# Softmax over 64 MB: stores moved to Pool's software descriptors, with each engine's share of a store requested as one packet

## Chip, cores, metric

One core of a Trainium2 chip. The metric is device time in microseconds of one execution. "Span" is the profiled time from the first to the last instruction, some 2 us shorter. DVE is VectorE, ACT is ScalarE, Pool is GpSimd and SP is SyncE.

## The reference, cut

```python
x = randn(32, 512, 1024), float32;  temperature = 0.5
scaled  = x / temperature
shifted = scaled - max(scaled, axis=-1)
out     = exp(shifted) / sum(exp(shifted), axis=-1)
```

That is 16384 rows of 1024 elements, 67.11 MB in and 67.11 MB out.

## The kernel before

The rows form 16 tiles of 4.19 MB (128 partitions x 8 rows x 1024 elements). In DRAM the 8 rows of a partition are adjacent, so each partition moves 32 KB in one piece. Six buffers hold tiles; the result overwrites the input in place, and a buffer is loaded anew when its store has landed. Each tile is computed as two groups of four rows.

```python
def load():                       # issued by SP, hardware descriptors
    i = len(tiles)
    if i < len(TILES):
        xt = data.tile([P, sum(TILES[i]), d], f32, name="xt")
        nc.sync.dma_start(out=xt, in_=dram(xf, i))                    # L61
        tiles.append(xt)
# maximum(g): DVE tensor_reduce (L70) and bias (L73); exponential(g): ACT (L79)
# divide(g):  DVE reciprocal (L91) and four tensor_scalar_mul (L93)
def store(g):                     # issued by ACT, hardware descriptors
    i, _, _, part = groups[g]
    if part:                      # after the second group of a tile
        a, k = part
        nc.scalar.dma_start(out=dram(of, i)[:, a : a + k, :],
                            in_=tiles[i][:, a : a + k, :])            # L101
        if a + k == sum(TILES[i]):
            load()
# ... cut ...
for _ in range(BUFS): load()      # BUFS = 6
for g in range(len(groups) + 1):
    if g < len(groups): maximum(g); exponential(g)
    if g > 0:           divide(g - 1); store(g - 1)
```

## Time and profile before

| quantity | before |
|---|---|
| time, median | 318.2 us |
| span | 316.0 us |
| DVE, ACT busy | 75%, 47% |
| DMA queues q1 (loads), q10 (stores) | 49.7%, 49.2% of 16 engines |
| store and load, issue to landing, median | 38.6 us, 50.2 us |

The last row of the table is longer than the 9.7 us that a tile takes at the plateau of 433 GB/s: loads and stores are in flight together and several of each are queued (a store is issued every 19.4 us in the middle of the kernel and takes 38.6 to land). The busy digits of the page, the queue shares and the end of the timeline stand in the prediction, with their reading.

### The profile page before, as it was taken

What the parts mean: (1) busy time and instruction counts of PE and PEld (TensorE: products, weight loads), DVE (VectorE), ACT (ScalarE), POOL (GpSimd) and SP (SyncE); (2) the same over time, 40 slices, a digit from 0 to 9 for tenths busy, and PEclk for the clock granted to TensorE, in tenths of its full rate; (3) what the DMA queues carried; (4) which work ended last, traced back from release to release, by engine and by line L of the source; (5) the groups of instructions that cost most, each with busy time, mean ns of one, the idle gap of its engine ahead of it and who ended that gap; (6) DMA issues with size and microseconds to landing.
All of it is one profiled execution on the core that took longest, in us unless ns stands there. A gap on an engine that the chain in (4) does not pass through costs nothing.

```text
span 316.0 us, 620 instructions
## 1 busy us (share of the span) xinstructions
DVE 235.5 (75%) x224; ACT 149.6 (47%) x257; POOL 0.2 (0%) x4
## 2 busy tenths in 40 slices
DVE  0399999999689494994949859497693976949720
ACT  0176666666526255361554605546064560645500
POOL 0000000000000000000000000000000000000000
DMA  8999999999999999999999999999999999999996
GB/s 332 411 452 423 373 460 415 452 425 431 436 427 440 427 444 423 444 419 448 415 452 411 452 408 456 423 444 427 436 431 432 440 423 444 419 444 419 452 411 274
DMA packets 4612, 134.25 MB, mean 425 GB/s; under 512 B 512, under 2 KB 512, under 8 KB 512
## 3 DMA queue, kind: packets, MB, share of 16 engines
q1 hardware_dynamic: 2304, 67.11, 49.7%
q10 hardware_dynamic: 2304, 67.11, 49.2%
q14 instruction: 4, 0.03, 0.0%
HBM read 67.11 MB, written 67.11 MB: 425 GB/s over the span
## 4 chain that ended last, share of the span: by engine, by line
DVE 49%; DMA 32%; another core or an unknown queue 9%; ACT 5%; issue 1%; DVEq 0%; SPq 0%
DVE top L70 29%; DMA xt<-in_x_dram 20%; DVE xt L93 18%; DMA out_dram<-xt 12%; ACT xt L79 5%; DVE recip L91 1%; DVE bias L73 1%; DVEq L147 0%; SPq L61 0%
## 5 line engine op out<-in xcount | busy, mean ns | idle before, releaser
L79 ACT ACTIVATE xt<-xt,bias 128x1024 f32<-128x1024 f32 x128 | 145.4, 1137 | 136.8 <-DVE recip L91 119.4
L70 DVE TENSOR_REDUCE top<-xt 128x4 f32<-128x4096 f32 x32 | 141.3, 4416 | 62.6 <-DMA xt<-in_x_dram 62.6
L93 DVE TENSOR_SCALAR xt<-xt,recip 128x1024 f32<-128x1024 f32 x128 | 87.7, 749 | 1.1
L79 ACT ACTIVATION_READ_ACCUMULATOR xt<-xt,bias 128x1 f32 x128 | 23.9, 187 | 0.0
L79 ACT ACT_TABLE_LOAD x1 | 1.3, 1283 | 13.0 <-DMA xt<-in_x_dram 13.0
L91 DVE RECIPROCAL recip<-sums 128x4 f32<-128x4 f32 x32 | 5.5, 171 | 2.1 <-ACT xt L79 2.1
L73 DVE TENSOR_SCALAR bias<-top 128x4 f32<-128x4 f32 x32 | 5.4, 170 | 1.1
L133 POOL MEMSET const-bfloat16-1.0<- 128x1 bf16 x1 | 0.1, 101 | 0.0
L133 POOL MEMSET const-uint8-127<- 128x1 uint8 x1 | 0.1, 101 | 0.0
L133 POOL MEMSET const-float32-0.0<- 128x1 f32 x1 | 0.1, 98 | 0.2 <-issue 0.2
L133 POOL MEMSET const-float32-1.0<- 128x1 f32 x1 | 0.1, 98 | 0.0
## 6 DMA issues: line engine op xcount, KB each, us to landing
xt<-in_x_dram SPq DMA_DIRECT2D x16, 4096.0 KB, 50.2
out_dram<-xt ACTq DMA_DIRECT2D x16, 4096.0 KB, 38.6
```

Source lines behind the costliest of these rows:

```text
L70: nc.vector.tensor_reduce(out=top, in_=tiles[i][:, a : a + k, :], axis=mybir.AxisListType.X, op=extreme)
L73: nc.vector.tensor_scalar_mul(bias, in0=top, scalar1=-scale)
L79: nc.scalar.activation(tiles[i][:, a + b, :], tiles[i][:, a + b, :], mybir.ActivationFunctionType.Exp, bias=bias[:, b : b + 1], scale=scal ...
L91: nc.vector.reciprocal(recip, sums)
L93: nc.vector.tensor_scalar_mul(tiles[i][:, a + b, :], in0=tiles[i][:, a + b, :], scalar1=recip[:, b : b + 1])
L133: nc = _bacc.Bacc("TRN2", target_bir_lowering=False, num_devices=1)
```

## The change

Words used here: a descriptor is one contiguous piece of a transfer; a packet is one entry of the trace's packet records, one or more descriptors that an engine moves together; a ring is what one queue has waiting on one engine; framing is the request for one packet (`single_packet=True`). The intent: take the stores off ACT's queue, and let each DMA engine drain its share of a store without handing over to the loads in between, so that buffers come free sooner.

```diff
-            nc.scalar.dma_start(out=dram(of, i)[:, a : a + k, :], in_=tiles[i][:, a : a + k, :])
+            nc.gpsimd.dma_start(out=dram(of, i)[:, a : a + k, :], in_=tiles[i][:, a : a + k, :], single_packet=True)
```

## The prediction

> **What bounds the kernel now.** I read the page of the profile first: the busy digits per slice, then the DMA queues.
>
> ```profile
> span 316.0 us, 620 instructions
> DVE 235.5 (75%) x224; ACT 149.6 (47%) x257; POOL 0.2 (0%) x4
> DMA  8999999999999999999999999999999999999996
> DMA packets 4612, 134.25 MB, mean 425 GB/s; under 512 B 512, under 2 KB 512, under 8 KB 512
> q1 hardware_dynamic: 2304, 67.11, 49.7%
> q10 hardware_dynamic: 2304, 67.11, 49.2%
> ```
>
> No engine is full, but the 16 DMA engines are at 9 tenths or more in every slice but the first and the last. Loads (q1) and stores (q10) fill 49.7% + 49.2% = 98.9% of 316 us, or 312.5 us. Of the 4612 packets, 512 are tiny (semaphore increments) and 4 belong to an instruction queue; the other 4096 carry 134.2 MB, so 32 KB each, 256 per engine. 312.5 / 256 is 1.22 us per packet (the packet records say 1.213 for nearly all). Next, the view by windows, which gives the rate in each stretch (columns: window, length, DVE, ACT and POOL busy, PE clock, DMA share, GB/s):
>
> ```profile
> 0.00:8.00 8.00, 0.00 (x0) 0.00 (x0) 0.20 (x4) 1.00 0.85 328
> 160.00:200.00 40.00, 30.17 (x30) 19.27 (x35) 0.00 (x0) 1.00 1.00 433
> 290.00:300.00 10.00, 7.99 (x10) 6.60 (x12) 0.00 (x0) 1.00 1.05 452
> 313.00:316.00 3.00, 0.00 (x0) 0.00 (x0) 0.00 (x0) 1.00 0.05 22
> ```
>
> The plateau is 433 GB/s, so one tile one way (4.19 MB) costs 4.19/0.433 = 9.7 us, and 32 of them 310 us. The first window lacks (433-328)/433 x 8 = 1.9 us (issue and first byte), the last about 2.9 us. 310 + 1.9 + 2.9 = 315 of 316. The kernel is transfers back to back, with no hole to remove. Last, the timeline of the end:
>
> ```profile
> 282.62 4.42 DVE L70 TENSOR_REDUCE top<-xt 128x4 f32<-128x4096 f32 x1 [4.50 <-DMA xt<-in_x_dram]
> ...
> 290.13 0.34 ACTq L101 DMA_DIRECT2D out_dram<-xt  x1
> ...
> 299.61 2.74 DVE L93 TENSOR_SCALAR xt<-xt,recip 128x1024 f32<-128x1024 f32 x4
> 302.38 0.34 ACTq L101 DMA_DIRECT2D out_dram<-xt  x1
> ```
>
> The last load lands at 282.6. The store of tile 14 is issued 7.5 us later and that of tile 15 19.8 us later. Yet the DMA never pauses: at 282.6 some 120 of 134 MB have moved, and the remaining 3.3 stores need 32 us. That backlog of stores is what hides the last tile's computation, and it exists because loads and stores share the engines evenly, so stores are always late:
>
> ```profile
> xt<-in_x_dram SPq DMA_DIRECT2D x16, 4096.0 KB, 50.2
> out_dram<-xt ACTq DMA_DIRECT2D x16, 4096.0 KB, 38.6
> ```
>
> A store takes 38.6 us from issue to landing, four times its 9.7 us of work: half rate, two outstanding.
>
> [...] the packet records alternate between q1 and q10 once both have work, and the first store (issued at 32.7, first packet 37.1) takes 18.8 us for its 9.7 us of data. [...] The trace of before has no software descriptors[...]; it does show L93 at 1024 elements in 749 ns and L70 at 4096 in 4416 ns, 1.37 against 0.93 per ns[...]. [...] Here the first load was issued at 0.7 and the first window lacks 1.9, so about 1.2 us by hardware[...].
>
> **The change part by part.** *Removed:* 16 issues on ACT's queue, 338 ns each, 5.4 us. ACT is 47% busy and waits for DVE (119.4 us before L79), so nothing is gained. Nor do stores become ready earlier: at 62.19 the divide ended and at 62.22 ACT issued. *Added:* 16 issues on Pool, which is otherwise empty. The instruction order shows each waiting for the same DVE count, DVE and SP otherwise in the same order. Each store is ready as a divide ends, and the next DVE instruction is the 4.42 us maximum of L70[...]; descriptor writing should fit in there. After the last store DVE is idle. [...] I reckon only a later start of 0.5 to 2 us per store, hidden by queued loads everywhere but at the end. *Moved:* who gets the engines. Each engine's share of a store is 8 descriptors of 32 KB. As one packet, it is served whole: 9.7 us undisturbed instead of 19 us alternating. The stores jump the queue, landing after about 12 to 16 us (9.7 + software start[...]: the first store of before waited 4.4 us[...]) instead of 38.6. Buffers come free earlier, but only so that loads wait in the queue instead: the DMA has work all the time, and the middle of the kernel keeps its 19.4 us per tile.
>
> The end does not. All loads together with all stores but those of the last two tiles are 30 transfers, 30 x 9.7 = 291 us, so the last load lands around 292 rather than 282.6, with little left to do beside the computation. From its start on DVE, store 14 is issued at +7.5 and store 15 at +19.8. What is idle then depends on how far earlier stores have got:
> - All earlier stores done, DVE waiting for the load: idle for 7.5 + 1.5 until store 14 starts, and 19.8 - 7.5 - 9.7 = 2.6 between the two. Sum 11.6 us: 318.2 + 11.6 = 330.
> - The last two loads land 9.7 us apart, as a late store start allows: tile 14 starts at 0, tile 15 lands at 9.7 while DVE is busy until 14.8 (2 x 7.39 per tile). Store 13, issued at 7.5, runs 9.7 to 19.4. Store 14 is issued at 14.8 + 7.5 = 22.3, starts at 23.8 (idle 4.4) and ends at 33.5; store 15 is issued at 14.8 + 19.8 = 34.6 and starts at 36.1 (idle 2.6). Sum 7.0: 325.
> - Another store (12) still unfinished when the last load lands: the 4.4 goes, 2.6 plus about 0.5 to 1 of software start remains: 321 to 322.
>
> Tile by tile from 32.7 on, with DVE needing 14.8 per tile and DMA 19.4, which of the three comes out turns on one or two us of store start-up. I can't fix that from the trace of before, so the middle is predicted.
>
> **The rivals.** *Framing does nothing:* if the packet is split, or loads slip in anyway, the sharing stays even, the store backlog stays, and only the last store's slower start shows: 318 to 319. [...] here one would have 256 KB; no run so far shows one. *Software descriptors become the bound:* if writing one store's takes longer than 4.4 us[...]: 328 to 335. The idle Pool and the long L70 speak against it. *Faster:* [...] prompt stores free buffers sooner. But [...] no load is late for want of a buffer in a way that leaves the DMA idle; 317 at best.
>
> **Range and chances.** Framing without effect 0.12 (318.5), the case with 2.6 to 3.5 idle 0.33 (321.5), the case with 7 idle 0.33 (325), the case with 11.6 idle 0.13 (330), a descriptor penalty 0.07 (332), a gain 0.02 (317). The weighted mean is 38.2 + 106.1 + 107.3 + 42.9 + 23.2 + 6.3 = 324. The 2% line lies at 324.6, inside the third case. So faster 0.02, within 2% 0.50, slower 0.48; 8 in 10 within 319 to 330.
>
> **What will show each step right or wrong.** Right: a software queue takes the place of q10 with 67.11 MB, store landing drops from 38.6 to 12 to 16 us, and loads wait longer than 50.2; the plateau stays 433 in windows of 40 us from 100 to 280; the last load lands near 287 to 292; and a hole shows in the DMA digits of the last three slices, before and between the last two stores. The L70 and L93 durations stay at 4416 and 749 ns. Wrong: store landing still near 38 us (no framing), a plateau below 425 (software descriptors cost throughput), or DVE durations growing[...]. A result under 317 would refute the claim that the DMA engines set the floor.

Passages that no trace or run of this case shows are cut from this text, and the cuts are marked. Terms of its sums went with them; the sums themselves stand as recorded:

- The store landing of 12 to 16 us contained, beside 9.7 us of data and the software start, a wait of some 3.4 us, the author's estimate of a part of the measured 4.4.
- The "1.2 us by hardware" runs from the issue of the first load to its first data. The start of a software store was not shown: the trace before has no software descriptors. The 0.5 to 2 us of later start, the 1.5 us between issue and start of a store in the cases that came to 325 and 330, and the 0.5 to 1 us in the case of 321 to 322 are estimates.
- The rival of 328 to 335 came to 2 to 4 us on top of the cases, for a collision of issues with divides that no trace had shown.
- The 317 "at best" came to 318.2 less 1.6 us, for a ceiling of the rate that no trace shows.

The last three are in the weighted mean of 324. That a store requested as one packet is served whole, on which the three cases rest, was an assumption too; no trace had shown it.

## The result, and the profile after

The changed kernel took 318.1 us (median of four runs, 317.96 to 318.24) against 318.19 for the kernel before. The ratio is 1.000, with a 95% interval of 0.9985 to 1.0015. Ratios in this document are the mean time of one kernel's runs over that of the other's runs of the same rounds, so not quite the ratio of the medians that are quoted. Executions over 1.5% slower than the fastest of the same kernel are left out of the means. The time is below the range of 319 to 330 that was on record.

The page of the changed kernel, where the same parts as before are shown (busy shares, DMA digits, packets, queues):

```profile
span 316.5 us, 639 instructions
DVE 235.5 (74%) x224; ACT 149.6 (47%) x257; POOL 8.8 (3%) x20
DMA  8999999999999999999999999999999999999995
DMA packets 4612, 134.25 MB, mean 424 GB/s; under 512 B 512, under 2 KB 512, under 8 KB 512
q1 hardware_dynamic: 2304, 67.11, 49.6%
q0 software_dynamic: 2304, 67.11, 49.1%
```

The change is really in: q0, a software queue, has taken the place of q10, and Pool has 16 instructions more. The rest is a copy. The number of packets is the same to the unit, the DMA digits are full from the second slice on, and there is no hole in the last ones. The issues of the changed kernel, with size and median time to landing, say the same:

```profile
xt<-in_x_dram SPq DMA_DIRECT2D x16, 4096.0 KB, 49.1
out_dram<-xt POOLq DMA_DIRECT2D x16, 4096.0 KB, 39.2
```

A store still takes 39.2 us to land. It was to fall to 12 to 16. The groups of the changed kernel (line, engine, operation, shapes, count | busy, mean ns | idle before and what ended it) show what the new instruction costs:

```profile
L70 DVE TENSOR_REDUCE top<-xt 128x4 f32<-128x4096 f32 x32 | 141.3, 4416 | 61.4 <-DMA xt<-in_x_dram 61.4
L93 DVE TENSOR_SCALAR xt<-xt,recip 128x1024 f32<-128x1024 f32 x128 | 87.7, 749 | 1.1
...
L101 POOL DMA_DIRECT2D out_dram<-xt x16 | 8.6, 540 | 293.0 <-DVE xt L93 293.0
```

Pool spends 540 ns on each store, and the two DVE groups have exactly their durations of before. The end of the changed kernel's timeline (start, length, instruction):

```profile
281.49 4.42 DVE L70 TENSOR_REDUCE top<-xt 128x4 f32<-128x4096 f32 x1 [4.51 <-DMA xt<-in_x_dram]
...
289.26 0.53 POOL L101 DMA_DIRECT2D out_dram<-xt  x1 [18.85 <-DVE xt L93]
...
301.52 0.53 POOL L101 DMA_DIRECT2D out_dram<-xt  x1 [11.72 <-DVE xt L93]
```

The last load lands at 281.5 (before: 282.6), and the last two stores are issued 7.8 and 20.0 us later (before: 7.5 and 19.8). There is one engine less to wait for and one generator more, and both kernels run the same course to within about a microsecond.

So the question is not where the time went, but why the store did not get ahead of the loads. Two answers are possible. Either the request for one packet has no effect on what the DMA engines see, or the engines do not take turns packet by packet. A second question is whether the rest of the prediction, that stores served first would cost time at the end, was right at all. The experiments take these in turn.

### The profile page after: what moved, and what is told of

It reads as the page before. It is cut to its first block, busy times and chain, and to the rows that moved or that the text cites. A ratio compares the mean times of both kernels' runs of the same rounds, so it can differ in the third digit from the quotient of the medians.

```text
span 316.5 us, 639 instructions
## 1 busy us (share of the span) xinstructions
DVE 235.5 (74%) x224; ACT 149.6 (47%) x257; POOL 8.8 (3%) x20
## 3 DMA queue, kind: packets, MB, share of 16 engines
q1 hardware_dynamic: 2304, 67.11, 49.6%
q0 software_dynamic: 2304, 67.11, 49.1%
HBM read 67.11 MB, written 67.11 MB: 424 GB/s over the span
## 4 chain that ended last, share of the span: by engine, by line
issue 89%; DMA 4%; POOL 2%; POOLq 0%
DMA xt<-in_x_dram 4%; POOL out_dram L101 2%; POOLq L147 0%; POOLq L101 0%
## 5 line engine op out<-in xcount | busy, mean ns | idle before, releaser
L70 DVE TENSOR_REDUCE top<-xt 128x4 f32<-128x4096 f32 x32 | 141.3, 4416 | 61.4 <-DMA xt<-in_x_dram 61.4
L93 DVE TENSOR_SCALAR xt<-xt,recip 128x1024 f32<-128x1024 f32 x128 | 87.7, 749 | 1.1
L101 POOL DMA_DIRECT2D out_dram<-xt x16 | 8.6, 540 | 293.0 <-DVE xt L93 293.0
## 6 DMA issues: line engine op xcount, KB each, us to landing
out_dram<-xt POOLq DMA_DIRECT2D x16, 4096.0 KB, 39.2
```

Of the source, the lines that this page charges most:

```text
L70: nc.vector.tensor_reduce(out=top, in_=tiles[i][:, a : a + k, :], axis=mybir.AxisListType.X, op=extreme)
L93: nc.vector.tensor_scalar_mul(tiles[i][:, a + b, :], in0=tiles[i][:, a + b, :], scalar1=recip[:, b : b + 1])
L101: nc.gpsimd.dma_start(out=dram(of, i)[:, a : a + k, :], in_=tiles[i][:, a : a + k, :], single_packet=True)
```

## The experiments

For the question of turns I read the trace's packet records (queue, start and size of each) in a stretch where both rings have work, and counted store packets and load packets. All counts are in one table, after the runs have been introduced; they leave out the 4-byte packets that report a completion. In the comments of the diffs, e1 to e11 number the runs.

### Framing left out

```diff
-            nc.gpsimd.dma_start(..., single_packet=True)
+            nc.gpsimd.dma_start(...)
```

> Stores by Pool, framing left out (32 KB descriptors as before). If the framing had no effect on this transfer (theory A) the run repeats the changed kernel: 318.1 us within 0.3%, store landing 39.2 us, last load landing near 281.5 us of the span. If the framing did something that a second effect cancelled (theory B), taking it out moves the time or the landing: over 1% or over 5 us of landing.

Measured: 318.22 us, ratio 1.0009 (0.9994 to 1.0024). The store landing is 39.6 us, and there are again 2048 store packets of 32 KB. Theory A holds: for this transfer the framing changes nothing that a run shows, and no second effect hides behind it. Moving the stores to Pool costs nothing either.

### Store descriptors of 8 KB, with framing and without

A cap on the contiguous piece makes each partition's 32 KB four descriptors of 8 KB, 32 per engine and store. The loads keep 32 KB.

```diff
-            nc.gpsimd.dma_start(..., single_packet=True)
+            nc.gpsimd.dma_start(..., single_packet=True, max_dma_last_dim=8192)   # e2
+            nc.gpsimd.dma_start(..., max_dma_last_dim=8192)                       # e3
```

> Stores by Pool with framing, each descriptor capped at 8 KB (32 per engine and store), loads left at 32 KB. Theory A1 (an engine takes turns between rings descriptor by descriptor, whatever the framing): stores get 8 KB for each 32 KB of load while both wait, one fifth, so store landing rises from 39.2 us to 45 us or more and loads land sooner than 49 us. Theory A2 (framing is honoured, but a packet with 256 KB in 32 KB descriptors is cut into pieces): the 8 KB descriptors travel together, at least 32 KB per turn, so landing is 39 us or less. Theory A3 (packet of all 32 served whole): landing 12 to 16 us and time 320 to 330 us.

> The same without framing. Under A1 it equals the run with framing, in time (within 0.3%) and landing (within 2 us). Under A2 or A3 it differs from it: here one fifth for the stores, landing 45 us or more, there much less.

Measured: 324.14 us with framing (ratio 1.0195) and 324.09 us without (1.0196). First the issues of the run with framing, then those of the run without:

```profile
xt<-in_x_dram SPq DMA_DIRECT2D x16, 4096.0 KB, 18.2
out_dram<-xt POOLq DMA_DIRECT2D x16, 4096.0 KB, 56.2
```

```profile
xt<-in_x_dram SPq DMA_DIRECT2D x16, 4096.0 KB, 18.0
out_dram<-xt POOLq DMA_DIRECT2D x16, 4096.0 KB, 56.3
```

The two agree within 0.2 us. Stores have become slow (56 us) and loads fast (18 us), as theory A1 has it where a turn gives a store 8 KB and a load 32 KB. A2 and A3 fall at this size: no group of 8 KB descriptors travelled together. Both runs are 6 us slower than the kernel before: from 160 to 240 us they move 419 and 420 GB/s against 433. Why is left open.

### Still smaller descriptors

In the runs so far every data packet was one descriptor, of 32768 or 8192 bytes. These runs ask what happens below 8 KB. Stores are cut into quarters of two rows (2 KB descriptors, 32 per engine) or eighths of one row (1 KB, 32 per engine).

```diff
-            nc.gpsimd.dma_start(out=dram(of, i)[:, a : a + k, :], in_=tiles[i][:, a : a + k, :], single_packet=True)
+            for b in range(a, a + k, 2):                      # e11: step 1, rows b : b + 1
+                nc.gpsimd.dma_start(                          # e10: nc.scalar
+                    out=dram(of, i)[:, b : b + 2, :], in_=tiles[i][:, b : b + 2, :],
+                    max_dma_last_dim=2048,                    # e11: 1024
+                    single_packet=True)                       # e6 and e11; not in e7 and e10
```

> Each store cut into four of 1 MB by Pool, 2 KB descriptors (32 per engine, 64 KB[...]), framed; loads at 32 KB. If framing works where the descriptors are short (theory A2), an engine serves 64 KB of store for 32 KB of load: a 1 MB store lands in under 20 us and loads land in 45 us or more. If turns go by descriptor whatever the framing (A1), stores get 2 KB for 32 KB, one seventeenth, until the buffers run out: loads land within 20 us and a store in 45 us or more.

> The same without framing. A1: equal to the framed one within 0.5% in time and within 3 us in both landings. A2: clearly different landings.

> Stores in quarters at 2 KB, but by ACT through the hardware queue. The Pool runs show store packets of 4096 bytes in the records (16384 of them), so two descriptors to a packet. If that pairing is the software generator's own framing, the hardware queue shows 32768 store packets of 2048 bytes, and the stores get 2 KB instead of 4 KB for each 32 KB of load: while both wait, about 26 GB/s against about 48. If the records merely merge neighbours, the hardware run shows 4096 bytes too.

> Stores in eighths by Pool with framing, 1 KB descriptors, 32 per engine and store (32 KB). If framing were acted on wherever the descriptors are few and short, the records show store packets of 32768 bytes and even turns with the loads. If the generator keeps to 4096 bytes whatever is asked, they show packets of 4096 bytes, four descriptors each, and stores get 4 KB for 32 KB of load. If framing went by descriptor, packets of 1024.

Measured: 344.79 us with framing (median of three runs, 340.76 to 345.12, ratio 1.078; a fourth of 345.91 counts as slow) and 341.52 us without (340.39 to 342.45, ratio 1.074). The medians are 1% apart where I had expected 0.5%, but the ranges overlap and so do the intervals; the landings agree within 0.4 us (41.3 and 40.9 for stores, 18.7 and 18.5 for loads). The store landing meets neither expectation: A2 said under 20 us, A1 45 us or more. The single look at ACT's quarters took 341.2 us, that at the eighths 361.3 us. Why these kernels are 7 to 14% slower was not followed up; they serve only to show the packets. The queue lines of the page, in the order of the framed quarters, the unframed quarters, ACT's quarters and the framed eighths (queue, kind, packets, MB, share), where 1024, 1024, 1024 and 2048 packets are the semaphore increments (16 for each store):

```profile
q0 software_dynamic: 17408, 67.11, 49.6%
```

```profile
q0 software_dynamic: 17408, 67.11, 50.3%
```

```profile
q10 hardware_dynamic: 33792, 67.11, 51.9%
```

```profile
q0 software_dynamic: 18432, 67.12, 51.9%
```

Without the increments that is 16384, 16384, 32768 and 16384 data packets for 67.11 MB, so 4096, 4096, 2048 and 4096 bytes each. In the Pool runs the software generator did pack: two descriptors of 2 KB, or four of 1 KB, to a packet. But its packets came to 4096 bytes in all three, whether one packet was asked for (quarters and eighths) or not (quarters), where framing as asked would have made 64 KB or 32 KB. The hardware queue gave each of ACT's 2 KB descriptors a packet of its own. Records do not just merge neighbours, or the hardware run would show 4096 as well.

Now the counts of packets that began in a stretch where both rings had work:

| run | stretch, us of the span | store packets | load packets | bytes of a store packet / load packet |
|---|---|---|---|---|
| before | 44 to 56 | 80 | 80 | 32768 / 32768 |
| changed kernel | 44 to 56 | 80 | 80 | 32768 / 32768 |
| framing left out | 44 to 56 | 80 | 80 | 32768 / 32768 |
| stores 8 KB, framed | 44 to 56 | 144 | 128 | 8192 / 32768 |
| stores 8 KB, unframed | 44 to 56 | 144 | 128 | 8192 / 32768 |
| quarters 2 KB by Pool, framed | 44 to 56 | 144 | 142 | 4096 / 32768 |
| quarters 2 KB by Pool, unframed | 44 to 56 | 144 | 144 | 4096 / 32768 |
| quarters 2 KB by ACT | 78 to 86 | 94 | 95 | 2048 / 32768 |
| eighths 1 KB by Pool, framed | 44 to 56 | 144 | 142 | 4096 / 32768 |
| loads 8 KB, stores by ACT (below) | 38 to 46 | 90 | 88 | 32768 / 8192 |

In all these stretches the turns are one packet each, with packets from 2048 to 32768 bytes. In the two rows of 144 to 128 a load ended within the stretch; with its 16 completion packets, which the counts leave out, the loads have 144 too. With 16 engines, the edges of a stretch alone can shift a count by up to 16. By the counts, stores in packets of 2, 4, 8 and 32 KB beside loads of 32 KB got 24, 49, 98 and 218 GB/s. Where the software generator packed two descriptors of 2 KB into 4096 bytes, a store got 49 GB/s, and where the hardware queue did not, 24 GB/s: here the turn follows the packet and not the descriptor. This settles the first question for these transfers: turns go packet by packet. Whether a longer store packet would have had the engine for longer was not shown: none over 32 KB was ever formed. My theory A1, turns by descriptor, was too narrow: it cannot be told from turns by packet at 8 and 32 KB, where each descriptor is a packet, and at 2 KB by Pool it is wrong.

The same runs show something that the changed kernel does not: here many of Pool's issues run at the same time as the divides of L93. The durations of L93 (min/median/max in ns, first and last start), framed quarters by Pool first, then the quarters by ACT:

```profile
L93 DVE TENSOR_SCALAR xt<-xt,recip x128: 733/749/1002, 22.6 to 302.4; 128x1024 f32<-128x1024 f32 x128
```

```profile
L93 DVE TENSOR_SCALAR xt<-xt,recip x128: 744/749/755, 22.7 to 329.1; 128x1024 f32<-128x1024 f32 x128
```

In the framed quarters 47 divides overlap an issue on Pool, and 19 of these take over 800 ns; of the 81 others none takes over 754. Pool's issues take up to 1192 ns (the first 1313) where they overlap a divide, and at most 763 elsewhere. So in this run the two do hold each other up when they meet. In the changed kernel none of the 16 issues meets a divide.

### Priority for the stores by another way

In the runs above turns went by packet (144 store packets of 4096 bytes to 144 load packets of 32768 in the unframed quarters), so stores should get priority if the packets of the loads are made shorter. This does what the framing was to do, with ACT's hardware queue as before. The control makes both short, to keep the shares even.

```diff
-            nc.sync.dma_start(out=xt, in_=dram(xf, i))
+            nc.sync.dma_start(out=xt, in_=dram(xf, i), max_dma_last_dim=8192)        # e4 and e5
-            nc.scalar.dma_start(out=dram(of, i)[:, a : a + k, :], in_=tiles[i][:, a : a + k, :])
+            nc.scalar.dma_start(..., max_dma_last_dim=8192)                          # e5 alone
```

> The kernel before (stores by ACT, 32 KB descriptors) with the load descriptors capped at 8 KB. If turns go by descriptor, stores now get 32 KB for 8 KB of load: the priority that I had expected of the framing. Then store landing falls to 11 to 17 us and, if my account of the end was right, the backlog of stores is gone when the last load lands (at 285 to 292 us instead of 282.6), a hole of 3 to 11 us shows in the last 30 us, and the time is 321 to 330 us. If landing falls and no hole appears, the account of the end was wrong too. If landing stays at 38 us, turns do not go by descriptor.

> The kernel before with load and store descriptors both capped at 8 KB. Shares are even again, so under the account of turns by descriptor the store backlog and the busy end come back: store landing 37 to 42 us, last load landing with three stores to go, no hole. What stays is the cost of shorter descriptors alone; from the stores alone at 9.8 us a tile in the capped store runs against 9.7, I expect 321 to 326 us. If it were as slow as the run with capped loads alone (332), that run's loss would be the short descriptors and not the hole.

Measured: short loads alone 332.07 us (ratio 1.042), both short 321.39 us (1.010). In the first, stores land in 17.0 us; in the second, in 39.6, and it met its expectation. The DMA digits of the page, short loads alone first, then both short:

```profile
DMA  7999999999999999999999999999999999784877
```

```profile
DMA  7999999999999999999999999999999999999996
```

The hole of the prediction is there in the first, in the last six slices, and absent from the second. By windows (DMA share is the last figure but one), in the run with short loads alone:

```profile
282.00:330.00 48.00, 32.28 (x33) 18.55 (x32) 0.00 (x0) 1.00 0.74 317
302.00:306.00 4.00, 3.93 (x8) 2.99 (x5) 0.00 (x0) 1.00 0.00 0
```

(1 - 0.74) x 48 = 12.5 us idle, of which about 1 us is the close after the last packet; between 302 and 306 nothing moves while DVE is busy for 3.93 of 4 us with the last tiles. The gap to before, 332.1 - 318.0 = 14.1 us, is this hole and the price of short loads. The two were not separated exactly: the last 48 us of the kernel before have 2.4 us idle too (packet records), so some 10 us of the gap is the hole, and the other 4 or so are near the 3.3 us that short loads and stores together cost in the control. From 100 to 240 us the rate is 427 GB/s here, 428 in the control and 434 before. From 160 to 240 us it is 425 here and 428 in the control, against 419 with framed stores at 8 KB and loads at 32 KB; that run had its stores from Pool and these two from ACT, so the comparison is not clean, and the cause is open. The expectation missed in three places, each by little: the time is 2 us above its 330, the hole of about 11.5 is just above its 11, and the last load lands at 292.9, not by 292.

### Priority only at the end, and only before the end

```diff
-            nc.sync.dma_start(out=xt, in_=dram(xf, i))
+            nc.sync.dma_start(out=xt, in_=dram(xf, i), **({"max_dma_last_dim": 8192} if i >= 12 else {}))   # e8; e9: i < 12
```

> The kernel before with only the last four loads capped at 8 KB, so that stores get the priority only near the end. If the hole at the end is what cost most of the 14 us of the run with all loads capped, this run has it too (DMA digits below 9 in the last four slices, last load landing at 286 us or later) at hardly any cost of short descriptors: 321 to 330 us. If the loss was the short descriptors, it comes to a quarter of 14 us at most, 318 to 321.5 us, without a hole.

> The mirror of the run with the last four loads capped: the first twelve loads at 8 KB, the last four at 32 KB, stores by ACT at 32 KB. Stores have the priority through the middle of the kernel and even shares at the end. If only the state at the end counts, the backlog grows back during the last four loads, the hole shrinks to a few us, and the time is 319 to 323 us in spite of three times as many short descriptors. If priority in the middle is itself a loss, it is over 326.8 us, the time of the mirror.

Measured: with the last four loads short, 326.79 us, ratio 1.027 (1.0256 to 1.0287), within the 321 to 330 expected. The windows of the kernel before, then of this run:

```profile
270.00:312.00 42.00, 25.70 (x28) 16.51 (x30) 0.00 (x0) 1.00 1.00 432
```

```profile
282.00:322.00 40.00, 28.70 (x33) 18.55 (x32) 0.00 (x0) 1.00 0.78 333
296.00:300.00 4.00, 3.93 (x7) 2.10 (x3) 0.00 (x0) 1.00 0.02 8
```

Before, the engines are full to the end. Here (1 - 0.78) x 40 = 8.8 us are idle, and the time is 326.8 - 318.1 = 8.7 us longer. Over the last 48 us of each run the packet records have 2.4 us idle before and 10.3 here, so the hole is some 8 of the 8.7 us. In this run the last load's completion increments come between 284.5 and 287.8, against 279.8 to 282.1 before.

With the first twelve loads short and the last four long: 324.95 us, ratio 1.021, against 319 to 323 expected. The backlog of stores did not grow back fully within four loads: when the last load lands, 2.7 stores are still to be moved, against 3.3 before and 3.0 in the mirror run. In the window from 282 to 323 the share is 0.84, so 6.6 us are idle, about 0.8 us of it the close. The hole is smaller than in the mirror run but not a few us, and the statement that only the last four loads matter is too strong; the run does bear out that priority in the middle, where the engines stay full, is not itself dearer than at the end.

## Why the prediction was wrong

**What bounds the kernel: right.** The sum of 310 us of transfers, 1.9 us of start and 2.9 us of close describes the changed kernel as well; its plateau from 160 to 240 us is again 433 GB/s. Nothing went under 317 us.

**What was removed: right.** ACT's 5.4 us of issue were worth nothing.

**What was added: right, and cheap.** Issue on Pool is 531 ns (667 the first time), well inside the 4.4 us of the maximum that follows. L70 and L93 kept 4416 and 749 ns: 15 of the 16 issues fall within a maximum of L70 and the last comes after the last divide, as the prediction had it, so no hold-up of the one by the other could show. (In the framed quarters, divides that met an issue took up to 1002 ns and the others at most 754.) The shortest time from issue to landing of a store rose from 12.8 to 13.5 us: 0.7 us, within the 0.5 to 2 us that I had estimated for a later start, and it left the time where it was.

**What was moved: this is the step that failed.** It says: "As one packet, it is served whole: 9.7 us undisturbed instead of 19 us alternating." The runs show that the store's share was not one packet. With 32 KB descriptors it was eight, with framing and without; the turns stayed 80 to 80, and a store still took 39.2 us to land instead of 12 to 16. I took the framing named in the change for a fact about what the engines would receive, and went on to work out the consequences of that. The evidence against it was in my own list of rivals, "Framing does nothing", with the remark that no run so far showed a packet of 256 KB, and I gave it 0.12. It was what happened.

**The end: right as a conditional.** Given priority for the stores, I had foreseen a last load around 287 to 292, a hole before and between the last two stores, and 321 to 330 us. The runs that made the priority by shorter load packets show 326.8 us with a hole of 8.8, and 332.1 us with about 11.5 and short descriptors besides. The three cases of the prediction (idle 3, 7, 11.6 us) span the first and nearly the second. These runs test the priority by other means; in no run was a store's whole share served in one turn.

**The chances.** "Within 2%" at 0.50 was right by luck more than by reason: most of that weight stood for a hole of 3 us, and there was none. The range from 319 left out exactly the rival that came true, whose own estimate was 318.5.

**What stays open.** Why the request for one packet had no effect: whether the generator on this system never heeds it for a plain copy, or heeds it under a condition that none of the shapes tried here met (32, 8, 2 and 1 KB descriptors; 8 to 32 descriptors and at least 32 KB per engine and store). It was not lost on the way into the program: when the framed kernels are built again, the built program has the request on every store (16, 16, 64 and 128 of them) and on no load. No run asked for one packet on ACT's hardware queue.

No experiment pointed to a kernel faster than both: each one that changed the shares or shortened the descriptors lost, and at 433 GB/s the unchanged transfers leave little to take out (310 of 316 us).

## What to carry to other kernels

Before predicting from what an option is called, ask which count or size in the trace would differ if it were acted on, and keep the case "it is not" at a good weight until a run has shown it. Two streams on the same DMA engines shared them packet for packet here, so the sizes of the packets set who got how much: stores in packets of 4096 bytes beside loads of 32768 got 49 GB/s, stores of 32768 bytes 218. At 8 and 32 KB a packet was one contiguous piece, whichever engine issued it; at 2 KB it depended on the issuer, since Pool's pieces were joined to 4096 bytes and ACT's were not. In this kernel, which is bound by transfers, a backlog of stores at the end was useful: 3.3 stores left when the last load landed filled the engines while the last tile was computed, and serving stores early at the end (last four loads short) moved that computation into the open: a hole of some 8 us, and 8.7 us more time.
